# FFN gate and up, conv inputs, stick-breaking queries and keys and all gates with both activation parts as one 512-column operand

## The chip, the cores and the metric

The kernel runs on one core of one Trainium2 chip. The metric is device time in microseconds (us) of a launch; a profile is a separate, recorded execution. TensorE (PE) multiplies, with weight loads of its own (PEld); VectorE (DVE) and ScalarE (ACT) work element by element; GpSimd (POOL) does little here; SyncE (SP) and ScalarE issue the DMA transfers. Each engine takes its instructions in the order that was written into its stream when the program was built.

## What is computed

Two layers of an encoder on 256 rows of 1024 channels, all in float32. Each layer is an FFN, a mixer of three branches, and a second FFN, each followed by a residual and a layer norm:

```python
for l in range(2):
    x = layernorm(ALPHA * x + 0.5 * swiglu(x, ffn1_w_in[l], ffn1_w_out[l]))   # d_ff 2816
    x = layernorm(ALPHA * x + mixer(x, l))
    x = layernorm(ALPHA * x + 0.5 * swiglu(x, ffn2_w_in[l], ffn2_w_out[l]))

def swiglu(x, w_in, w_out):
    gate, up = split(x @ w_in)
    return (silu(gate) * up) @ w_out

def mixer(h):
    qa, ka, va, zb, xbc, dtb, qc, kc, vc, gpre = split(h @ w_in)
    o_a = diff_attention(qa, ka, va)              # two softmax maps a head
    o_b = mamba2(zb, silu(conv4(xbc)), dtb)       # state-space scan (SSD)
    o_c = stick_breaking(qc, kc, vc)
    return sum(sigmoid(gpre[r] + bias[r]) * (o[r] @ w_branch[r]) for r in 0, 1, 2) @ w_out
```

## The kernel before

Matrix products are made nearly in float32 from a faster format, float32r. A weight and an activation are each split into a high and a low part, and three products are added: high·high, high·low, low·high (`passes`). Weights come from DRAM 1 MB at a time (SP's queue, two `raw` buffers); ScalarE makes the high half (line 93), VectorE the low half (line 94), into six pairs of buffers `whi`, `wlo` (pool `wsp`). The transposed activations of a sub-layer lie in `xThi` and `xTlo`, 8 blocks k of 256 columns each.

`gemm_s` (line 131) makes a 128 x 256 piece of a transposed product: for each of 8 k, three matmuls of 256 columns with the weights as stationary operand. The FFN's `part_s` calls it for gate and up (4 FFNs x 10 blocks j x 2 x 2 halves f), `block_s` (line 372) for the six blocks of convolution inputs, for four blocks of queries and four of keys of the stick-breaking branch, and for 12 gate blocks a layer; `proj` calls it for the branch projections, with other activations. `block_a` (line 362) and `part_a` use xT the other way round, as the stationary operand, with 512 (line 368) or 256 (line 275) columns of weights moving. The FFN's output product (line 308) has `hhi`, `hlo` as stationary operand and 512 columns of weights moving.

Tiles are placed back to back in a partition. Those of weights, of `hhi` and `hlo` have sizes that are multiples of 64 floats, so they start on one grid of 256 bytes. `new_xT` takes a slice that begins `APART` = 48 floats into its tile, and the mixer's first small tile, `ss`, of 48 floats, shifts the mixer's tiles by as much.

PSUM has eight banks of 512 float32 columns: two in pool `gm`, four in `at`, two in `tp`. A bank is handed to the next user when the one before has read it. A `gemm_s` block takes one `gm` bank for both halves. The pool `at` holds the accumulators of the FFN's output and of the mixer's output, and in between the small products of the SSD stage (lines 452 to 521), the scores of stick-breaking (line 551) and of differential attention (line 629).

The order of instructions on each engine is set when the program is built, by a planner with costs of its own; it may move a block ahead of others if its buffers are free. In the SSD stage softplus gives `dt` and `dta` (lines 441 to 450); lines 454 to 457 make cumulated decays in an `at` bank; line 459 copies them, line 461 writes them to DRAM, line 464 reads them back to all partitions, one transfer of 1 MB for each half c of the rows; line 496 (16 times a half) and line 500 make decay factors, line 501 multiplies, and lines 507 and 512 are the matmuls.

## Time and profile before

| | |
|---|---|
| time, median of 3 runs | 1610.74 us (1610.71 to 1612.2) |
| profiled execution | 1617.37 us, span 1615.6 us, mean granted TensorE clock 0.994 |
| PE, PEld busy | 1591.5 us (99%), 1467.2 us (91%) |
| DVE, ACT busy | 984.7 us (61%), 848.4 us (53%) |
| matmuls, weight loads | 11282 each |

The span is the time from the first to the last instruction. A busy share says in how much of the span at least one instruction of the engine was running. The length of one matmul has its way through the array in it, so that matmuls that follow one another overlap, and what one costs is read from the distance of the starts. An arrow "<-" behind an idle time names what ended it.

### The profile page before, as it was taken

The page shows a single profiled execution, that of the slowest core. Times are in us where ns is not written, and L with a number is a line of the kernel's source. Part 1 is how long each engine was busy: PE and PEld are TensorE (multiplying, and loading weights), DVE is VectorE, ACT ScalarE, POOL GpSimd, SP SyncE. Part 2 cuts the span into 40 slices and gives each one's busy share as a digit, 9 for nine tenths or more (in the row PEclk, how much of TensorE's full clock was granted, in tenths as well). Part 3 has the DMA queues.
Part 4 walks back from the last instruction along what each step waited for, and adds up shares of the span by engine and source line. Part 5 has one row for each costly group of instructions (what it writes and reads, how often), then busy time and mean ns, then how long its engine had stood idle before and what let it go on. Part 6 is the DMA issues. An engine that isn't in the chain of part 4 may idle for free.

```text
span 1615.6 us, 26930 instructions
## 1 busy us (share of the span) xinstructions
PE 1591.5 (99%) x11282; PEld 1467.2 (91%) x11282; DVE 984.7 (61%) x1510; ACT 848.4 (53%) x1285; POOL 17.6 (1%) x28
## 2 busy tenths in 40 slices
PE   8999999999999999999999999999999999999998
PEld 8999899888799998999899998998788999999997
DVE  5555657767585556455655565777576855565454
ACT  5545356568675444444444453654676755444451
POOL 0000000000000000000000000000000000000000
PEclk9999999999999999999999999998999999999999
DMA  8665445543435674566445562663443356545651
GB/s 286 198 226 192 158 157 175 187 161 105 157 106 174 217 235 140 175 216 225 157 162 203 209 230 85 208 190 128 154 140 124 129 194 216 191 157 183 235 196 39
DMA packets 222117, 283.55 MB, mean 176 GB/s; under 512 B 8658, under 2 KB 185644, under 8 KB 221996
## 3 DMA queue, kind: packets, MB, share of 16 engines
q1 hardware_dynamic: 213676, 277.61, 51.0%
q10 hardware_dynamic: 8320, 4.23, 0.9%
q8 instruction: 88, 1.44, 0.4%
q14 instruction: 33, 0.27, 0.0%
HBM read 280.74 MB, written 1.08 MB: 174 GB/s over the span
## 4 chain that ended last, share of the span: by engine, by line
PE 95%; DVE 2%; DMA 2%; ACT 1%; issue 0%; POOL 0%; DVEq 0%; POOLq 0%; ACTq 0%
PE gm L135 52%; PE at L308 15%; PE gm L368 14%; PE gm L275 3%; PE at L730 2%; DMA t<-acd 2%; PE at L633 1%; PE at L507 1%; PE at L585 1%; PE at L577 1%; PE at L555 1%; PE tp L614 0%; DVE wlo L94 0%; DVE at L169 0%; DVE xt L160 0%; PE tp L145 0%
## 5 line engine op out<-in xcount | busy, mean ns | idle before, releaser
L94 DVE TENSOR_TENSOR wlo<-raw,whi 128x1024 fp32r<-128x1024 f32 x412 | 501.2, 1223 | 360.5 <-ACT whi L93 350.4
L93 ACT CAST whi<-raw 128x1024 fp32r<-128x1024 f32 x412 | 429.4, 1051 | 391.0 <-PE gm L135 229.4
L135 PE MATMUL gm<-xThi,whi 128*128 128x256 f32 x2112 | 595.1, 282 | 0.0
L135 PE MATMUL gm<-xTlo,whi 128*128 128x256 f32 x2112 | 594.8, 282 | 0.0
L135 PE MATMUL gm<-xThi,wlo 128*128 128x256 f32 x2112 | 594.2, 281 | 0.0
L135 PEld LDWEIGHTS gm<-xThi,wlo 128*128 128x128 f32 x2112 | 403.8, 191 | 1.8 <-issue 1.8
L135 PEld LDWEIGHTS gm<-xThi,whi 128*128 128x128 f32 x2112 | 398.4, 189 | 3.4 <-issue 1.8
L135 PEld LDWEIGHTS gm<-xTlo,whi 128*128 128x128 f32 x2112 | 397.9, 188 | 3.0 <-issue 1.6
L135 PE MATMUL gm<-t,whi 128*128 128x256 f32 x768 | 138.7, 282 | 0.0
L368 PE MATMUL gm<-whi,xThi 128*128 128x512 f32 x320 | 128.7, 402 | 1.2 <-ACT xThi L128 1.2
L94 DVE TENSOR_TENSOR wlo<-rawo,whi 128x1024 fp32r<-128x1024 f32 x68 | 83.1, 1225 | 72.8 <-ACT whi L93 69.7
L368 PE MATMUL gm<-whi,xTlo 128*128 128x512 f32 x320 | 126.9, 398 | 0.0
L368 PE MATMUL gm<-wlo,xThi 128*128 128x512 f32 x320 | 126.4, 395 | 0.0
L135 PEld LDWEIGHTS gm<-t,whi 128*128 128x128 f32 x768 | 117.2, 188 | 2.7 <-issue 2.7
L93 ACT CAST whi<-rawo 128x1024 fp32r<-128x1024 f32 x68 | 71.3, 1052 | 76.8 <-PE at L308 63.7
L135 PE MATMUL gm<-t,wlo 128*128 128x256 f32 x384 | 108.1, 281 | 0.0
L308 PE MATMUL at<-whi,hhi 128*128 128x512 f32 x256 | 78.9, 390 | 0.0
L308 PE MATMUL at<-wlo,hhi 128*128 128x512 f32 x256 | 78.9, 390 | 0.0
L308 PE MATMUL at<-whi,hlo 128*128 128x512 f32 x256 | 78.9, 390 | 0.0
L135 PEld LDWEIGHTS gm<-t,wlo 128*128 128x128 f32 x384 | 73.1, 190 | 0.0
L368 PEld LDWEIGHTS gm<-whi,xThi 128*128 128x128 f32 x320 | 60.3, 188 | 13.9 <-ACT xThi L128 2.1
L368 PEld LDWEIGHTS gm<-whi,xTlo 128*128 128x128 f32 x320 | 60.2, 188 | 13.5 <-DVE xTlo L129 0.9
(235 smaller groups left out, 1870.5 us busy)
## 6 DMA issues: line engine op xcount, KB each, us to landing
raw<-in_w_mix_in_dram SPq DMA_DIRECT2D x92, 1024.0 KB, 5.1
raw<-in_ffn_w_in_dram SPq DMA_DIRECT2D x85, 1024.0 KB, 4.9
rawo<-in_ffn_w_out_dram SPq DMA_DIRECT2D x44, 1024.0 KB, 7.2
raw<-in_w_branch_dram SPq DMA_DIRECT2D x24, 1024.0 KB, 5.5
raw<-in_w_mix_out_dram SPq DMA_DIRECT2D x8, 1024.0 KB, 6.2
t<-acd ACTq DMA_DIRECT2D x4, 1024.0 KB
rawo<-in_ffn_w_in_dram SPq DMA_DIRECT2D x2, 1024.0 KB
gb<-in_ln_g_dram SPq DMA_DIRECT2D x4, 512.0 KB
```

Source lines behind the costliest of these rows:

```text
L93: act.copy(out=hi, in_=src)
L94: dve.tensor_sub(out=lo, in0=src, in1=hi.bitcast(F32))
L135: pe.matmul(out=ps_out, lhsT=a[:, f:f + n], rhs=b[:, k, :], start=first, stop=(k == KT - 1 and i == 2))
L275: pe.matmul(out=ps[:, u * 256:(u + 1) * 256], lhsT=a[:, k, t * P:(t + 1) * P], rhs=c, start=first, stop=(k == KT - 1 and i == 2))
L308: pe.matmul(out=accs[t][h], lhsT=a[:, f, t * P:(t + 1) * P], rhs=c[:, h * 512:(h + 1) * 512], start=(j == 0 and f == 0 and i == 0), stop=( ...
L368: pe.matmul(out=ps, lhsT=a[:, k, t * P:(t + 1) * P], rhs=c, start=(k == 0 and i == 0), stop=(k == KT - 1 and i == 2))
L507: pe.matmul(out=py[:, 64 * h:64 * h + 64], lhsT=m[:, hh, :], rhs=xdt[:, c, 64 * hh:64 * hh + 64], start=True, stop=True)
L555: pe.matmul(out=pz[h][:, 0:S], lhsT=kcT[r, hp, 0:P], rhs=qcT[r, hp, :], start=True, stop=False, skip_group_check=True)
L577: pe.matmul(out=pz[h][:, 0:384], lhsT=trin, rhs=part[:, hs], start=False, stop=False, skip_group_check=True)
L585: pe.matmul(out=pz[c0][64 * h:64 * h + 64, 384:512], lhsT=vct[:, k, 64 * hh:64 * hh + 64], rhs=sp[:, 384 * h + c1:384 * h + c1 + P], start ...
L633: pe.matmul(out=pm[m][:, c:c + n], lhsT=qaT[r, h, t * P:(t + 1) * P], rhs=kaT[r, h, 0:n], start=True, stop=True, skip_group_check=True)
L730: pe.matmul(out=accs[t][h], lhsT=a[:, k, t * P:(t + 1) * P], rhs=c[:, h * 512:(h + 1) * 512], start=(k == 0 and i == 0), stop=(k == KT - 1 ...
```

## The change

`new_xT` makes one tile `xTj` in which, for each k, the 256 high columns and the 256 low columns stand side by side; it starts at offset `XPART` = 0, on the grid of the weights. A new `gemm_j` multiplies whi with all 512 columns at once, into a whole bank (left half high·high, right half high·low), and adds wlo times the 256 high columns to the left half. The two halves f of a block so take a bank each. ScalarE copies the right half out of PSUM (times a scale), VectorE adds the left half. The second bank comes from `tp` in the FFN's up and in the gates of branch 0, and from `at` in the convolution inputs, the queries, the keys and the other gates. What read PSUM directly (Silu, Tanh, the convolution's first tap, the product with up) reads the sum in SBUF. `block_a`, `part_a` and the dt product use the same tile as before, through its two views; `proj` still calls `gemm_s`.

```diff
@@ -31,6 +31,8 @@
 HOLD = 3
 
 APART = 48
+
+XPART = 0
 OFF_QA, OFF_KA, OFF_VA, OFF_ZB, OFF_XBC, OFF_DTB, OFF_QC, OFF_KC, OFF_VC, OFF_G = (
     0, 1024, 2048, 3072, 4096, 5632, 5648, 6672, 7696, 8720)
 NEG = -float(2 ** 100)
@@ -136,6 +138,14 @@
                           start=first, stop=(k == KT - 1 and i == 2))
                 first = False
 
+    def gemm_j(w, f, xT, ps):
+        for k in range(KT):
+            pe.matmul(out=ps, lhsT=w[k][0][:, f:f + P], rhs=xT[2][:, k, :], start=(k == 0), stop=(k == KT - 1),
+                      skip_group_check=True)
+            pe.matmul(out=ps[:, 0:S], lhsT=w[k][1][:, f:f + P], rhs=xT[0][:, k, :], start=False, stop=(k == KT - 1),
+                      skip_group_check=True)
+        return ps
+
 
     def transposed(t, xT):
         for q in range(2):
@@ -147,11 +157,9 @@
             split_act(xT[0][:, 4 * q:4 * q + 4, t * P:(t + 1) * P], xT[1][:, 4 * q:4 * q + 4, t * P:(t + 1) * P], pv)
 
     def new_xT():
-        def part(name):
-            whole = keep.tile([P, KT * S + 128], F32R, name=name)
-            return whole[:, APART:APART + KT * S].rearrange("p (k c) -> p k c", c=S)
-
-        return part("xThi"), part("xTlo")
+        whole = keep.tile([P, KT * 2 * S + 128], F32R, name="xTj")[:, XPART:XPART + KT * 2 * S]
+        both = whole.rearrange("p (k i c) -> p k i c", i=2, c=S)
+        return both[:, :, 0, :], both[:, :, 1, :], whole.rearrange("p (k c) -> p k c", c=2 * S)
 
     def layernorm(t, accs, coef, gb, sq):
         st = sm.tile([P, 5], F32, name="st")
@@ -289,15 +297,21 @@
                 spare = fresh and j == 1
                 wg = load_cols(w_in[l], j * 256, None, raws[0] if spare else None)
                 wu = load_cols(w_in[l], FF + j * 256, None, raws[1] if spare else None)
-                pg, pu = gm_tile(), gm_tile()
                 hT = new_h()
+                sg = fp.tile([P, 512], F32, name="h")
                 for f in range(2):
-                    gemm_s(pg[:, f * S:(f + 1) * S], wg, f * P, xT)
-                sg = fp.tile([P, 512], F32, name="h")
-                act.activation(out=sg, in_=pg, func=AF.Silu)
+                    ps = gemm_j(wg, f * P, xT, gm_tile())
+                    sf = sg[:, f * S:(f + 1) * S]
+                    act.copy(out=sf, in_=ps[:, S:2 * S])
+                    dve.tensor_add(out=sf, in0=sf, in1=ps[:, 0:S])
+                act.activation(out=sg, in_=sg, func=AF.Silu)
+                su = fp.tile([P, 512], F32, name="h")
                 for f in range(2):
-                    gemm_s(pu[:, f * S:(f + 1) * S], wu, f * P, xT)
-                dve.tensor_mul(out=sg, in0=sg, in1=pu)
+                    ps = gemm_j(wu, f * P, xT, tp_tile())
+                    sf = su[:, f * S:(f + 1) * S]
+                    act.copy(out=sf, in_=ps[:, S:2 * S])
+                    dve.tensor_add(out=sf, in0=sf, in1=ps[:, 0:S])
+                dve.tensor_mul(out=sg, in0=sg, in1=su)
                 split_act(hT[0], hT[1], sg.rearrange("p (f c) -> p f c", c=S))
                 return hT
 
@@ -369,12 +383,13 @@
                                       start=(k == 0 and i == 0), stop=(k == KT - 1 and i == 2))
                     evac(t, ps)
 
-            def block_s(c0, evac, w=wm):
-                ws = load_cols(w, c0)
-                ps = gm_tile()
+            def block_j(c0, dst, scale=1.0, second=at_tile):
+                ws = load_cols(wm, c0)
                 for f in range(2):
-                    gemm_s(ps[:, f * S:(f + 1) * S], ws, f * P, xT)
-                evac(ps.rearrange("p (f c) -> p f c", c=S))
+                    ps = gemm_j(ws, f * P, xT, second() if f else gm_tile())
+                    act.mul(out=dst[:, f, :], in_=ps[:, S:2 * S], mul=scale)
+                    dve.scalar_tensor_tensor(out=dst[:, f, :], in0=ps[:, 0:S], scalar=scale, in1=dst[:, f, :],
+                                             op0=ALU.mult, op1=ALU.add)
 
             ss = mp.tile([P, APART], F32, name="ss")[:, 0:2 * 8].rearrange("p (t h) -> p t h", h=8)
             zs = slot("t1", [P, NT, D])
@@ -406,14 +421,14 @@
             bcF = mp.tile([P, 4, S], F32, name="bcF")
             last_silu = [None]
             for cc in range(6):
-                def evac(ps, cc=cc):
+                def conv(cc=cc):
                     pad = mp.tile([P, 768], F32, name="w3", bufs=4)[:, 0:2 * 259].rearrange("p (f c) -> p f c", c=259)
                     ac = mp.tile([P, 768], F32, name="w3", bufs=4)[:, 0:512].rearrange("p (f c) -> p f c", c=S)
                     dve.memset(pad[:, :, 0:3], 0.0)
-                    act.copy(out=pad[:, :, 3:259], in_=ps)
+                    block_j(OFF_XBC + 256 * cc, pad[:, :, 3:259])
                     for f in range(2):
                         c = 2 * cc + f
-                        act.activation(out=ac[:, f, :], in_=ps[:, f, :], func=AF.Identity,
+                        act.activation(out=ac[:, f, :], in_=pad[:, f, 3:259], func=AF.Identity,
                                        scale=v[:, 36 + c:37 + c], bias=v[:, 48 + c:49 + c])
                         for i in range(3):
                             dve.scalar_tensor_tensor(out=ac[:, f, :], in0=pad[:, f, i:i + S],
@@ -429,7 +444,7 @@
                             pe.transpose(out=pt[:, t * S + f * P:t * S + (f + 1) * P],
                                          in_=ac[:, f, t * P:(t + 1) * P], identity=ident)
                     act.copy(out=xs[:, :, cc * 256:(cc + 1) * 256], in_=pt.rearrange("p (t c) -> p t c", c=256))
-                block_s(OFF_XBC + 256 * cc, evac)
+                conv()
 
 
             pt = tp_tile()
@@ -540,8 +555,8 @@
 
 
             for cc in range(4):
-                block_s(OFF_QC + 256 * cc, lambda ps: act.mul(out=qcT[:, 2 * cc:2 * cc + 2, :], in_=ps, mul=0.125))
-                block_s(OFF_KC + 256 * cc, lambda ps: act.copy(out=kcT[:, 2 * cc:2 * cc + 2, :], in_=ps))
+                block_j(OFF_QC + 256 * cc, qcT[:, 2 * cc:2 * cc + 2, :], 0.125)
+                block_j(OFF_KC + 256 * cc, kcT[:, 2 * cc:2 * cc + 2, :])
             for h in range(2):
                 block_a(OFF_VC + 512 * h, lambda t, ps: act.copy(out=vct[:, t, 512 * h:512 * h + 512], in_=ps))
 
@@ -691,12 +706,10 @@
 
             def gate(r, dp):
                 gt = slot(("bcF", "xde")[(r + dp) % 2 if r else dp % 2], [P, 2, S])
-
-                def evac(ps):
-                    for f in range(2):
-                        kk = 60 + 8 * r + 2 * dp + f
-                        act.activation(out=gt[:, f, :], in_=ps[:, f, :], func=AF.Tanh, scale=0.5, bias=v[:, kk:kk + 1])
-                block_s(OFF_G + 1024 * r + 256 * dp, evac)
+                block_j(OFF_G + 1024 * r + 256 * dp, gt, 1.0, at_tile if r else tp_tile)
+                for f in range(2):
+                    kk = 60 + 8 * r + 2 * dp + f
+                    act.activation(out=gt[:, f, :], in_=gt[:, f, :], func=AF.Tanh, scale=0.5, bias=v[:, kk:kk + 1])
                 return gt
 
             def proj(r, dp, o, gt, first, final=None):
```

The order of TensorE changes most behind layer 0's convolution inputs. Before, behind the SSD's decay products (lines 454 to 457, then 486 and 487), queries and keys follow (`gm_2969` and on):

```order
L457 MATMUL at_2657<-tri_sb_872,dta_2648 16x128 x2
L486 MATMUL at_2681<-bcF_2187 128x256
L487 MATMUL at_2681<-bcF_2187 128x128
L486 MATMUL at_2687<-bcF_2187 128x256
L487 MATMUL at_2687<-bcF_2187 128x128
L135 MATMUL gm_2969<-xThi_1945,wlo_2962 128x256
L135 MATMUL gm_2969<-xThi_1945,whi_2965 128x256
L135 MATMUL gm_2969<-xTlo_1946,whi_2965 128x256
```

180 rows of line 135 stand between that last line 487 and the first line 507. In the changed program (where lines 454, 457, 486, 487, 507 and 512 are now 469, 472, 501, 502, 522 and 527) the same place reads:

```order
L472 MATMUL at_2373<-tri_sb_787,dta_2364 16x128 x2
L501 MATMUL at_2397<-bcF_1975 128x256
L502 MATMUL at_2397<-bcF_1975 128x128
L501 MATMUL at_2403<-bcF_1975 128x256
L502 MATMUL at_2403<-bcF_1975 128x128
L522 MATMUL at_2428<-t3_1819,t4_1820 128x64 x8
L522 MATMUL at_2443<-t3_1819,t4_1820 128x64 x8
L522 MATMUL at_2474<-t3_1819,t5_1821 128x64 x8
L527 MATMUL at_2484<-xde_1823,cbm_2396 128x512
L522 MATMUL at_2494<-t3_1819,t5_1821 128x64 x8
L527 MATMUL at_2504<-xde_1823,cbm_2396 128x512
L143 MATMUL at_2584<-xTj_1734,whi_2557 128x512
```

Three first halves of queries and keys (`gm_2565`, `gm_2613`, `gm_2661`, 16 matmuls each) stand ahead of line 469, none between lines 502 and 522, and the second halves in `at` banks stand behind line 527; layer 1 has the same order.

On VectorE, the rows that lead up to the copy of the decays (line 459, now 474), before:

```order
L473 TENSOR_TENSOR t3_2031<-t2_2030,dt_2647 128x1024 x2
L94 TENSOR_TENSOR wlo_3082<-raw_3079,whi_3081 128x1024
L476 TENSOR_TENSOR t2_2030<-t2_2030,bvec0_894 128x1024
L94 TENSOR_TENSOR wlo_3086<-raw_3079,whi_3085 128x1024
L476 TENSOR_TENSOR t2_2030<-t2_2030,bvec0_894 128x1024
L459 COPY dtr_2663<-at_2657 16x256
```

and in the changed program, where line 391 adds a half-block's two parts:

```order
L464 SCALAR_TENSOR_TENSOR dt_2363<-dt_2363,dta_2364 128x32
L465 SCALAR_TENSOR_TENSOR dta_2364<-dt_2363,bvec0_809 128x32
L488 TENSOR_TENSOR t3_1819<-t2_1818,dt_2363 128x1024 x2
L391 SCALAR_TENSOR_TENSOR t6_1824<-gm_2661,t6_1824 128x256
L491 TENSOR_TENSOR t2_1818<-t2_1818,bvec0_809 128x1024
L474 COPY dtr_2379<-at_2373 16x256
```

Two splits of weights (line 94) are gone from there, and one add has come.

In the FFN the blocks of gate, up and output product follow one another as before, each half-block with 16 matmuls in place of 24.

## Rows read from the trace of the kernel before

**Rows 1.** The page, part 1: busy time of each engine, share of the span.

```profile
PE 1591.5 (99%) x11282; PEld 1467.2 (91%) x11282; DVE 984.7 (61%) x1510; ACT 848.4 (53%) x1285; POOL 17.6 (1%) x28
```

**Rows 2.** Groups by line and form: one pass of line 135, busy and mean ns.

```profile
L135 PE MATMUL gm<-xThi,whi 128*128 128x256 f32 x2112 | 595.1, 282 | 0.0
```

**Rows 3.** The timeline of PE in the first FFN: start, length, instruction.

```profile
29.55 0.28 PE L135 MATMUL gm<-xThi,whi 128*128 128x256 f32 x1
...
36.26 0.28 PE L135 MATMUL gm<-xThi,whi 128*128 128x256 f32 x1
```

**Rows 4.** The same in layer 0's convolution inputs.

```profile
243.42 0.28 PE L135 MATMUL gm<-xThi,whi 128*128 128x256 f32 x1
...
246.82 0.28 PE L135 MATMUL gm<-xThi,whi 128*128 128x256 f32 x1
```

**Rows 5.** The same in the FFN's output product.

```profile
188.56 0.39 PE L308 MATMUL at<-dhi,hhi 128*128 128x512 f32 x1
...
195.58 0.39 PE L308 MATMUL at<-dhi,hlo 128*128 128x512 f32 x1
```

**Rows 6.** The same in block_a, layer 0.

```profile
341.21 0.39 PE L368 MATMUL gm<-whi,xThi 128*128 128x512 f32 x1
...
348.08 0.39 PE L368 MATMUL gm<-whi,xThi 128*128 128x512 f32 x1
```

**Rows 7.** Busy us by stretch: PE, PEld, DVE, ACT, POOL; granted clock; DMA.

```profile
20.00:180.00 160.00, 160.00 (x1181) 152.24 (x1181) 90.34 (x99) 80.69 (x93) 0.00 (x0) 1.00 0.63 218
221.00:257.00 36.00, 36.00 (x319) 35.91 (x318) 26.70 (x48) 25.07 (x39) 0.00 (x0) 1.00 0.62 191
1093.90:1104.00 10.10, 10.10 (x50) 10.10 (x49) 10.10 (x15) 3.08 (x5) 0.00 (x0) 0.50 0.32 105
```

**Rows 8.** Groups by line: PSUM read of 256 columns by ACT, by DVE.

```profile
L538 DVE SCALAR_TENSOR_TENSOR t<-tp,pvec,t 128x256 fp32r<-128x256 f32 x16 | 7.0, 477 | 11.4 <-ACT t L537 11.4
...
L537 ACT ACTIVATE t<-tp,pvec 128x256 fp32r<-128x256 f32 x16 | 6.7, 473 | 6.6 <-PE tp L534 6.6
```

**Rows 9.** Timeline of PE around the state-space stage, layer 0.

```profile
270.30 0.52 PE L454 MATMUL at<-dta,tri_sb 128*128 128x16 f32 x4
...
272.70 0.39 PE L487 MATMUL at<-bcF 128*128 128x128 f32 x2
...
294.98 3.79 PE L507 MATMUL at<-t,t 128*128 128x64 f32 x32 [1.48 <-DVE t L501]
```

**Rows 10.** Timeline of DVE there.

```profile
267.47 0.19 DVE L450 SCALAR_TENSOR_TENSOR dta<-dt,bvec 128x32 f32<-128x32 f32 x1
267.58 2.35 DVE L473 TENSOR_TENSOR t<-t,dt 128x1024 f32<-128x1024 f32 x2
...
274.39 0.41 DVE L459 COPY dtr<-at 16x256 f32<-16x256 f32 x1
...
285.08 3.23 DVE L496 TENSOR_SCALAR t<-t,ac 128x128 f32<-128x128 f32 x16 [1.47 <-DMA t<-acd]
...
291.94 1.85 DVE L496 TENSOR_SCALAR t<-t,ac 128x128 f32<-128x128 f32 x9 [2.50 <-DMA t<-acd]
293.71 1.22 DVE L501 TENSOR_TENSOR t<-t,cbm 128x1024 f32<-128x1024 f32 x1
```

**Rows 11.** Timeline of ACT and its DMA queue there.

```profile
275.86 1.05 ACT L93 CAST whi<-raw 128x1024 fp32r<-128x1024 f32 x1 [5.24 <-PE gm L135]
275.87 0.35 ACTq L461 DMA_DIRECT2D acd<-dtr  x1
...
278.53 2.13 ACTq L464 DMA_DIRECT2D t<-acd  x2
```

**Rows 12.** Timeline of PE in the state-space stage, layer 1.

```profile
1092.83 6.17 PE L507 MATMUL at<-t,t 128*128 128x64 f32 x32 [1.59 <-DVE t L501]
...
1099.12 0.41 PE L135 MATMUL gm<-xThi,whi 128*128 128x256 f32 x1
...
1103.38 0.41 PE L135 MATMUL gm<-xThi,wlo 128*128 128x256 f32 x1
```

## The prediction

> **What bounds the kernel now.** I read the page first. TensorE is busy in 99% of the span [rows 1], its 11.3 thousand matmuls in one unbroken line: a microsecond that it works less, or stands still more, is a microsecond of the time, wherever it is. VectorE and ScalarE, at 61% and 53% [rows 1], have room, so I price their work only where TensorE waits for it.
>
> Since busy times of pipelined matmuls overlap, the cost of one is not its mean of 282 ns [rows 2] but the distance between starts, read off the timeline. The three-pass product (whi·hi, whi·lo, wlo·hi for each k, line 135) has two paces. In the FFN 57 matmuls start in 6.71 us, one every 117.7 ns [rows 3]; in the convolution inputs 30 start in 3.40 us, one every 113.3 ns [rows 4]. Of 512-column matmuls, 31 steps of the FFN's output product take 7.02 us, 226.5 ns each, twice 113.3 [rows 5]; 30 steps of the mixer's block_a take 6.87 us, 229.0 ns each [rows 6]. So 0.443 ns a column is the floor seen here, and something adds 4.4 ns in the FFN's three-pass product and 2.5 ns in block_a. What differs between these is placement: hhi, hlo and the output weights lie on one 256-byte grid, while xThi and xTlo lie 48 floats off the grid of the weights. The convolution inputs are off it too and run at the floor [rows 4], so the grid is one way to it, not the only one.
>
> **Gains.** The change makes of each k two matmuls in place of three: 512 columns, then 256. The columns stay the same, 768; a weights load and a start go. With xTj on the grid I take 226.5 for the 512 [rows 5] and 113.3 for the 256 [rows 4]: 226.5 + 113.3 = 339.8 ns, against 3 x 117.7 = 353.1, that is 13.3 ns for a triple. Of the 2112 triples [rows 2] 1280 are in the FFNs (4 x 10 j, gate and up, 2 f, 8 k): 17.0 us. Of the mixers' 832 the 448 of convolution, queries and keys are at 3 x 113.3 = 339.9 already and gain nothing; the 384 of the gates I read at the FFN's pace, 5.1 us. block_a now has its stationary operand on the grid: 960 x 2.5 ns = 2.4 us; line 275, read at 117.7 against 113.3 ns [rows 3, 4], 384 x 4.4 ns = 1.7 us. Together 26.2 us. No row shows a 256-column matmul on the grid with a full weights load beside it. If each load goes on costing 4.4 ns, a pair is 348.6 ns and the gain 4.5 ns x 1280 = 5.8 us. The bounds are 5.8 and 26.2; I take the upper one, since the 512-column rows on the grid show no excess at all.
>
> The Trainium skill (TensorE: Matmul & The Clock Gate, Back-to-back issue gap) gives a warm matmul N/2.4 + 2.5 ns, a fixed cost per instruction. By it a triple would be 327.6 ns, a pair 325.0, and the gain an estimated 2.5 ns x 2112 = 5.3 us. The trace differs: over N/2.4 512 columns lie 13.2 ns [rows 5] and 256 lie 6.6 ns [rows 4], an excess that grows with the columns. The sum goes by the rows.
>
> **Evacuations.** Each half-block now adds a ScalarE copy of 256 columns from PSUM and a VectorE add; the nearest rows are 473 and 477 ns [rows 8]. An FFN step j (96 matmuls of 117.7 ns and 24 of 226.5, 16.7 us [rows 3, 5]) gets four of each, 1.9 us on either engine; over 160 us of FFN VectorE is busy 90.3 and ScalarE 80.7 [rows 7], so they rise from 56% and 50% to some 68% and 62%, under TensorE, and the four banks of gate and up are wanted again only a step later. In the convolution stage VectorE has 26.7 of 36 us [rows 7] and gets 12 x 0.48 = 5.7 more, 32.4 of about 35: still covered, but barely. I cost these at nothing; with the cover gone it is 2 to 3 us a layer.
>
> **The wait that is added.** The second half of a queries or keys block now takes its PSUM bank from the pool `at`, which the state-space (SSD) stage uses ahead of it, so the block can't be finished before that stage. The rows of the order show it: before, 180 matmuls of line 135 stand between line 487 and the first line 507, which is 20.4 us at 113.3 ns, the stretch 273.1 to 293.5 in the trace [rows 9], and TensorE waits 1.48 us. In the changed program nothing stands there: line 502 is followed by line 522, which waits for decays that come over DRAM. How long, from rows:
>
> From the end of line 450 (267.66) VectorE does line 473 twice (2.35 us), one new add (0.48), line 476 (1.18) and the copy 459 (0.41) [rows 10]: 4.4 us. Before, two splits stood in between. The write to DRAM then goes at once; before, it stood behind a cast that waited 5.24 us for TensorE, and went 1.07 us after the copy [rows 11]. From its issue to the first line 496 is 275.87 to 285.08, 9.2 us [rows 10, 11]. Sixteen of line 496 take 3.23 us and line 501 takes 1.22. Sum 18.1 us, in which TensorE has lines 454 to 487, 270.30 to 273.09 [rows 9], 2.8 us. **It idles 15.3 us.** The second chunk's decays are there 6.86 us after the first's [rows 10]; its 13 + 1 operations put the second group of matmuls 10.7 us after that first landing, while the first group ends 6.4 after it: 4.3 us more idle, or 1.0 if the broadcast, without weight loads beside it, lands 3.3 us sooner; I take 3. Ahead of line 469 the filler (three half-blocks of 2.7 us) about covers the softplus chain; I take 0.5. That is 18.8 us a layer against 1.48 now: 17.3 more, 34.6 for both. All queued behind the waiting line 522 on TensorE, the half-blocks, the rest of queries and keys, then block_a, comes that much later, and nothing later has slack to give it back [rows 1]. Bounds: 13 to 22 us a layer.
>
> **The clock.** In layer 1 the granted clock was 0.50, the 1.2 GHz level, for 10.1 us from 1093.9 [rows 7], after a wait of 1.59 us: 32 records of line 507 took 6.17 us against 3.79 in layer 0, and 20 matmuls of line 135 took 4.26 us (213 ns each) against 2.27 [rows 9, 12]. That costs some 4.6 us now, in one layer of two. After 15 us of idle I expect it in both, through the SSD's 9.7 us of small matmuls (part of it inside the waits above) and the first dense work behind: 6 us a layer, 12 - 4.6 = 7.4 us more. Bounds: -4.6 (no drop at all) and 15.
>
> **Sum**, against the profiled execution: 1617.4 - 26.2 + 34.6 + 7.4 = 1633.2 us, 15.8 more. The median of the runs is 1610.7, 6.6 under the profiled one; I carry the difference over: **1626.5 us**.
>
> **Rivals.** *The pace doesn't follow the grid*: every load keeps its 4.4 ns, the gain is 5.8 us, and the time 1610.7 + 42.0 - 5.8 = 1646.9. For it: the FFN and the convolution inputs have the same placement and yet differ [rows 3, 4], so placement alone doesn't set the pace. Against it: on the grid the pace is twice the floor to 0.1 ns [rows 5]. The fixed cost that the Trainium skill gives (TensorE: Matmul & The Clock Gate, Back-to-back issue gap) would by an estimate end at about the same place. *The wait is short*: the broadcasts, alone on the DMA engines, land 3.3 us sooner, the second gap closes to nothing and the clock holds: idle 18.8 - 3.3 - 3 = 12.5 a layer, 11 more than now, and no drop in either layer: 22 - 4.6 - 26.2 = -8.8, 1601.9. It decides below 13.1 us of added wait and clock a layer. Against it: the chain of lines 459, 461, 464, 496, 501 is serial, and 15 us of idle hardly leave the clock alone. *The gates starve the differential attention too*: their second halves also take `at` banks, which the scores of the heads hold; TensorE is filled there with gates and projections now. If eight half-blocks (21.8 us a layer) come too late for half of their gaps, it adds 10 us a layer: 1646.5. Against it: first halves and projections stay early in the order.
>
> **How the numbers follow.** The forecast gets 0.62, pace 0.14, short wait 0.12, gates 0.10, others 0.02. The forecast's own range is 1614 to 1640 (gain 15 to 26, wait 15 to 20 a layer). To leave out no more than 2 in 10 it goes to 1606 and 1646. A difference of 0.2% (3.2 us) is about what a measurement of this kernel can tell from none. Faster: most of the short wait, 0.11. Within: 0.08, where its parts mix with the forecast. Slower: 0.81.
>
> **What would show it.** FFN starts 340 ns apart per pair (348 by the pace rival); block_a at 226.5; TensorE idle of 15 us before the first line 522 and 1 to 4 before the second, in both layers, put down to VectorE or the DMA; clock 0.50 there in both layers; no TensorE waits over 1 us in the FFNs. The prediction is wrong if the order's gap is filled by a chain under 12 us, or if the pair runs under 330 ns.

## The result, and the profile after

The changed kernel takes 1664.6 us (median of 4 runs, 1663.7 to 1667.8) against 1611.5 us of the kernel before on the same chip: ratio 1.033, 95% interval 1.031 to 1.035. It is slower, as forecast, but by 53 us where 15.8 were forecast, and outside the range. The profiled execution took 1664.81 us, with a span of 1662.7. Part 1 of its page, to be laid beside [rows 1]:

```profile
PE 1610.6 (97%) x9170; PEld 1382.5 (83%) x9170; DVE 1093.7 (66%) x1774; ACT 930.6 (56%) x1523; POOL 17.5 (1%) x28
```

2112 matmuls are gone, yet the busy time of TensorE has risen by 19 us, and its idle share of the span from 1% to 3%. Stage by stage (each from its first transpose of the residual stream to that of the next stage, us):

| stage | before | after |
|---|---|---|
| FFN 1, 2, 3, 4 | 191.2, 191.0, 188.6, 198.9 | 191.4, 192.7, 189.1, 199.3 |
| mixer, layer 0 and 1 | 418.2, 423.1 | 441.8, 444.3 |

The four FFNs, which were to give 17 us, give nothing (2.8 us longer). The mixers lose 44.8 us.

**The pace.** Timeline of PE in the changed kernel: first a stretch of the first FFN, 30 pairs from the first row to the second, then one of layer 0's convolution inputs, 9 pairs. They answer to [rows 3, 4]:

```profile
117.78 0.40 PE L143 MATMUL gm<-xTj,whi 128*128 128x512 f32 x1
...
128.38 0.40 PE L143 MATMUL tp<-xTj,whi 128*128 128x512 f32 x1
...
235.50 0.40 PE L143 MATMUL gm<-xTj,whi 128*128 128x512 f32 x1
...
238.63 0.39 PE L143 MATMUL at<-xTj,whi 128*128 128x512 f32 x1
```

10.60 us over 30 are 353.3 ns a pair in the FFN, to the nanosecond what three products of 117.7 took [rows 3]. In the convolution inputs 3.13 us over 9 are 347.8 ns, where three products took 3 x 113.3 = 339.9 [rows 4]. The pair at 339.8 ns, on which 22 of the 26.2 us of gain were built, is nowhere in this trace. In the pairs of the FFN the next start comes some 236 ns behind the 512-column product and 117 behind the 256-column one, in the convolution inputs 230 to 232 and 115 to 117: both are over the 226.5 and 113.3 of my sum. The two smaller gains part ways, in the next rows: block_a, whose stationary operand is now on the grid, makes 75 steps in 17.00 us, 226.7 ns against the 229.0 of [rows 6] (in the mean of all its steps 227.9 against 229.4); line 283 (line 275 before), also there, makes 18 in 2.16 us, 120.0 ns, slower than the 117.7 at which I had it.

```profile
339.37 0.39 PE L382 MATMUL gm<-wlo,xTj 128*128 128x512 f32 x1
...
356.37 0.39 PE L382 MATMUL gm<-wlo,xTj 128*128 128x512 f32 x1
```

```profile
17.68 0.28 PE L283 MATMUL gm<-wlo,xTj 128*128 128x256 f32 x1
...
19.84 0.28 PE L283 MATMUL gm<-wlo,xTj 128*128 128x256 f32 x1
```

**The wait.** Timelines of PE, of VectorE and of ScalarE's DMA queue around the state-space (SSD) stage of layer 0, answering to [rows 9 to 11] (the last column is the idle time before, and what ended it):

```profile
269.53 0.38 PE L502 MATMUL at<-bcF 128*128 128x128 f32 x2
283.36 10.84 PE L522 MATMUL at<-t,t 128*128 128x64 f32 x48 [13.45 <-DVE t L516]
...
298.47 0.80 PE L143 MATMUL at<-xTj,whi 128*128 128x512 f32 x1
```

```profile
270.62 0.41 DVE L474 COPY dtr<-at 16x256 f32<-16x256 f32 x1
...
278.95 3.22 DVE L511 TENSOR_SCALAR t<-t,ac 128x128 f32<-128x128 f32 x16 [2.70 <-DMA t<-acd]
282.09 1.22 DVE L516 TENSOR_TENSOR t<-t,cbm 128x1024 f32<-128x1024 f32 x1
```

```profile
271.06 0.35 ACTq L476 DMA_DIRECT2D acd<-dtr  x1
```

The chain is the one foretold: copy, write to DRAM, decays back (278.95 - 271.06 = 7.9 us, 9.2 were taken from before), sixteen subtractions, the mask, and only then TensorE. The idle is 13.45 us, not 15.3. Behind it TensorE has 68 small products in four groups, for 15.1 us. Until the clock rises they start 213 ns apart, against 110 to 112 at the full clock, with one pause of 0.3 us where I had put a second gap of 3. The list of waits of the whole execution has both layers in its first row, and nothing new behind it that is longer than 2.4 us in all:

```profile
PE at L522 <- DVE t L516: 26.8, 2, 13.5
...
PE tp L673 <- ACT cbm L672: 2.4, 2, 1.2
```

The same stage by windows, columns as in [rows 7], answering to its last row. First the idle, then the groups of SSD products:

```profile
266.97:283.37 16.40, 2.90 (x19) 2.34 (x19) 11.91 (x32) 2.76 (x5) 0.00 (x0) 0.68 0.47 129
283.37:297.80 14.43, 14.33 (x65) 13.14 (x66) 11.35 (x27) 3.56 (x6) 0.00 (x0) 0.54 0.01 2
```

The granted clock is at 0.50, the lower level of 1.2 GHz, from 272.8 to 296.7 in layer 0 and for 27.3 us from 1098.8 in layer 1.

**What a layer lost.** The queries and keys products that TensorE ran inside the SSD stage, by the windows of their line, before (columns: length, PE, PEld, clock, DMA, GB/s) and after:

```profile
270.30:306.60 36.30, 25.21 (x213) 24.29 (x211) 1.00 0.61 192
```

```profile
266.97:298.47 31.50, 0.00 (x1) 0.03 (x1) 0.62 0.25 68
```

Before, the stage took 36.3 us of which TensorE spent 25.2 on 213 products of queries and keys. Now it takes 31.5 us without one of them, and the 25.2 us are to be done behind it: 25.2 - (36.3 - 31.5) = 20.4 us. From the layer's start to the start of stick-breaking the two timelines differ by just that (-3.0 us up to the cumulative sums, +23.4 from there); the differential attention and the gates add 3.2, together the 23.6 us of layer 0.

### The profile page after: what moved, and what is told of

Read it like the earlier page. It is cut to its first block, busy times and chain, and to the rows that moved or that the text cites. A ratio compares the mean times of both kernels' runs of the same rounds, so it can differ in the third digit from the quotient of the medians.

```text
span 1662.7 us, 23327 instructions
## 1 busy us (share of the span) xinstructions
PE 1610.6 (97%) x9170; PEld 1382.5 (83%) x9170; DVE 1093.7 (66%) x1774; ACT 930.6 (56%) x1523; POOL 17.5 (1%) x28
## 4 chain that ended last, share of the span: by engine, by line
PE 94%; DVE 3%; DMA 1%; ACT 1%; issue 0%; POOL 0%; SPq 0%; DVEq 0%; POOLq 0%; ACTq 0%
PE gm L143 15%; PE at L322 14%; PE gm L382 14%; PE tp L143 10%; PE gm L137 8%; PE gm L145 7%; PE tp L145 5%; PE at L143 5%; PE gm L283 3%; PE at L145 3%; PE at L743 2%; PE at L522 2%; PE at L648 1%; PE at L600 1%; PE at L592 1%; DMA t<-acd 1%
## 5 line engine op out<-in xcount | busy, mean ns | idle before, releaser
L143 PE MATMUL gm<-xTj,whi 128*128 128x512 f32 x1056 | 376.9, 397 | 0.0
L145 PE MATMUL gm<-xTj,wlo 128*128 128x256 f32 x1056 | 297.4, 282 | 0.0
L143 PE MATMUL tp<-xTj,whi 128*128 128x512 f32 x704 | 250.2, 397 | 0.0
L143 PEld LDWEIGHTS gm<-xTj,whi 128*128 128x128 f32 x1056 | 198.3, 188 | 45.5 <-issue 0.7
L382 PE MATMUL gm<-whi,xTj 128*128 128x512 f32 x640 | 204.1, 396 | 0.7 <-ACT xTj L130 0.7
L145 PEld LDWEIGHTS gm<-xTj,wlo 128*128 128x128 f32 x1056 | 199.4, 189 | 1.9 <-issue 0.3
L145 PE MATMUL tp<-xTj,wlo 128*128 128x256 f32 x704 | 197.6, 281 | 0.0
L143 PEld LDWEIGHTS tp<-xTj,whi 128*128 128x128 f32 x704 | 132.2, 188 | 32.4
L145 PEld LDWEIGHTS tp<-xTj,wlo 128*128 128x128 f32 x704 | 133.0, 189 | 0.0
L143 PE MATMUL at<-xTj,whi 128*128 128x512 f32 x352 | 127.0, 400 | 0.8 <-ACT w L658 0.8
L95 ACT CAST whi<-rawo 128x1024 fp32r<-128x1024 f32 x68 | 71.3, 1051 | 19.2 <-PE at L322 15.1
```

The source lines that it names most:

```text
L95: act.copy(out=hi, in_=src)
L143: pe.matmul(out=ps, lhsT=w[k][0][:, f:f + P], rhs=xT[2][:, k, :], start=(k == 0), stop=(k == KT - 1), skip_group_check=True)
L145: pe.matmul(out=ps[:, 0:S], lhsT=w[k][1][:, f:f + P], rhs=xT[0][:, k, :], start=False, stop=(k == KT - 1), skip_group_check=True)
L382: pe.matmul(out=ps, lhsT=a[:, k, t * P:(t + 1) * P], rhs=c, start=(k == 0 and i == 0), stop=(k == KT - 1 and i == 2))
```

## The experiments

Times are medians, and each ratio is against the kernel before, run beside the kernel named.

### The wait: banks, order, engines, clock

**Only the banks undone, and only the banks done.** First the edit in the changed kernel (the keys likewise), then that in the kernel before, in block_s, whose bank is then at_tile for queries and keys and gm_tile else:

```diff
-                block_j(OFF_QC + 256 * cc, qcT[:, 2 * cc:2 * cc + 2, :], 0.125)
+                block_j(OFF_QC + 256 * cc, qcT[:, 2 * cc:2 * cc + 2, :], 0.125, gm_tile)
```

```diff
-                ps = gm_tile()
+                ps = bank()
```

> The changed kernel, only the second PSUM tile of the stick-breaking queries and keys blocks comes from the same pool as their first (gm) and no longer from the pool that the SSD tiles use, so that these blocks can stand in the program between the cumulative sums and the SSD products again. Theory 1 (the wait at the SSD and the half-rate clock behind it made the loss): the idle of 13.4 us ahead of the scores in each layer shrinks to at most 3 us, the granted clock stays at 1.00 there in layer 0, the stretch from the cumulative sums to stick-breaking falls from 92.0 us by 20 to 24 us in each layer, and the time is 1618 to 1626 us, still above the kernel before because the pairs' pace is unchanged at 352 ns. Theory 2 (the two-engine evacuations and the pace made the loss, the wait only uncovered slack): the idle shrinks but the time stays above 1645 us.

> The kernel before, only the PSUM tile of the stick-breaking queries and keys blocks comes from the pool of the SSD tiles (at). No operand, pace or evacuation changes. Theory 1 (bank choice alone makes the wait and the slow clock): idle of 13 to 14 us ahead of the scores in both layers, a half-rate stretch of some 24 us behind it, 20 to 24 us a layer, time 1651 to 1660 us. Theory 2 (the wait is short without the other parts of the change): under 1625 us.

The kernel before with nothing but its queries and keys on the other pool takes 1668.6 us, ratio 1.032 (1.029 to 1.036): the bank alone makes a loss as large as that of the whole change. (It moves more than the change did: there only the second half of each block takes an `at` bank, here the whole block.) Its list of waits in layer 0's stage:

```profile
PE at L507 <- DVE t L501: 11.8, 1, 11.8
PE at L454 <- DVE dta L450: 7.6, 1, 7.6
```

The changed kernel with these banks put back takes 1645.9 us, 1.019 (1.016 to 1.022): by the ratios some 23 us better, not 40. By its number that is the second theory's side, by 1 us; by its reason it is neither, since a wait is left, in the right place:

```profile
PE at L522 <- DVE t L516: 8.0, 1, 8.0
PE gm L143 <- DVE t L391: 1.1, 1, 1.1
```

The idle is down from 13.45 to 8.0 us and not to 3. In the order of that program 67 matmuls of the pairs stand between line 502 and the first SSD product, some 11.8 us at 176 ns, where before there were 180 of 113.3 ns, 20.4 us. A half-block of pairs fills a bank by itself, so that two banks of gm hold half as much of this work ahead; that is my reading of the order. The clock is at 0.50 there as well, for 13.7 us in layer 0 and 20.5 in layer 1.

**Queries and keys as before, the rest changed** (the keys likewise; block_s and its gm tile are those of the kernel before).

```diff
-                block_j(OFF_QC + 256 * cc, qcT[:, 2 * cc:2 * cc + 2, :], 0.125)
+                block_s(OFF_QC + 256 * cc, lambda ps: act.mul(out=qcT[:, 2 * cc:2 * cc + 2, :], in_=ps, mul=0.125))
```

> The changed kernel, but the stick-breaking queries and keys keep three products of 256 columns, one PSUM tile of gm and one evacuation on ScalarE, as before the change; conv inputs, gates and FFN keep the joint operand. Theory 1 (the whole loss hangs on the queries and keys: their banks, and the second evacuation on VectorE that queues behind the SSD's work): no idle over 2 us ahead of the scores, granted clock 1.00 there in layer 0, mixer stretches of 418 to 425 us as before, time 1612 to 1622 us. Theory 2 (conv inputs and gates cost the mixer as well): mixer stretches of 428 us or more, time above 1630 us.

1616.5 us, ratio 1.0040 (1.0025 to 1.0054), mixers 420.0 and 420.3 us, and no idle in the stage: the row of its window there has TensorE busy for all of 52 us at clock 1.00.

```profile
258.00:310.00 52.00, 52.00 (x425) 50.55 (x424) 43.59 (x86) 27.78 (x42) 0.00 (x0) 1.00 0.57 185
```

So some 47 of the 53 us (1.033 down to 1.004) hang on the queries and keys. And the rest of the change, conv inputs, gates and all FFNs on pairs, gives no gain: it stands 7 us behind. In this kernel the three products of queries and keys read the operand on the grid, 6 triples between these rows, 2.16 us or 120.0 ns a product:

```profile
268.74 0.40 PE L137 MATMUL gm<-xTj,whi 128*128 128x256 f32 x2
...
270.90 0.40 PE L137 MATMUL gm<-xTj,whi 128*128 128x256 f32 x2
```

Before the change these 768 took 114.7 ns in the mean (stretches of 113.4 and of 117.8), so they make 4 of the 7 us.

**Is it the evacuation on VectorE?** In the kernel before, half of each queries or keys block is evacuated by VectorE:

```diff
+            def two(dst, cc, ps, scale):
+                act.mul(out=dst[:, 2 * cc, :], in_=ps[:, 0, :], mul=scale)
+                dve.tensor_scalar(out=dst[:, 2 * cc + 1, :], in0=ps[:, 1, :], scalar1=scale, scalar2=None, op0=ALU.mult)
```

> The kernel before, but the evacuation of the stick-breaking queries and keys is shared: ScalarE takes the first 256 columns of a block, VectorE the other 256; banks, operands and products as before. Theory 1 (what is left of the loss when the banks are undone, some 12 us a layer, comes from an evacuation on VectorE that queues behind the SSD's work): idle of some microseconds ahead of the first SSD product or inside the queries and keys, and 8 us or more a layer, time 1625 to 1640 us. Theory 2 (the pairs' shorter cover and their place in the order make it): within 4 us of the kernel before.

1616.9 us, 1.0013 (0.9996 to 1.0030): no loss to be seen, so that an evacuation on VectorE doesn't by itself make what is left. The pairs' evacuation in two steps, ScalarE and then VectorE, was not tried alone; TensorE's waits for it with the banks put back are 2.4 us in all. The shorter cover remains, read from the order and not tested by itself.

**Is the slow clock a loss?** Extra products, their result unused, keep TensorE at work in the wait (first kernel, below, with FILL 12). The second kernel has three more ahead of each later group of SSD products; the order puts 15 into the wait and three each ahead of the second and the fourth group:

```diff
                     py = at_tile()
+                    if c == 0 and g == 0:
+                        idle = tp_tile()
+                        for i in range(FILL):
+                            pe.matmul(out=idle, lhsT=cbm[:, 0, 0, :], rhs=zs[:, 0, 0:512], start=True, stop=True)
```

> The changed kernel with 12 extra products (fp32, 512 columns, about 0.9 us each, their result unused) between the scores and the first SSD product of each layer, in the middle of the 13.4 us in which TensorE idles. Nothing that the kernel computes is changed. Theory 1 (the idle lets the clock fall to half, and the half-rate stretch of 24 to 27 us is a loss of its own): the clock stays at 1.00 there, and the time falls by 8 to 20 us, to 1645 to 1657 us, although TensorE does more work. Theory 2 (the half-rate stretch lies beside VectorE's work and costs nothing): within 3 us of 1664.6. If the added products outlast the wait, up to 3 us a layer slower.

> The changed kernel with extra products (fp32, 512 columns, unused result) both in the wait ahead of the first SSD product (15) and between the SSD's groups of products (3 ahead of the second and of the fourth), since with the wait alone filled the granted clock still fell to half during the groups. Nothing that the kernel computes is changed. If the half-rate stretch is a loss of its own, the clock stays at 1.00 through the groups and the time falls by 6 us or more below 1663. If the SSD's end is set by VectorE and the clock lies beside it, the time stays within 3 us of the changed kernel (or rises by what the added products outlast the waits, up to 4 us a layer) while the half-rate stretch goes.

The first takes 1663.3 us, 1.0337 (1.0321 to 1.0352), the second 1662.1, 1.0318 (1.0294 to 1.0341), against the change's own 1.033. In the first the clock still fell, to 0.50 for 17.1 us from the SSD products on, in each layer. Windows and the end of the stage in the second:

```profile
270.00:285.00 15.00, 13.51 (x34) 6.18 (x33) 10.51 (x35) 2.77 (x5) 0.00 (x0) 1.00 0.51 141
285.00:299.00 14.00, 14.00 (x82) 10.19 (x80) 11.43 (x23) 4.28 (x8) 0.00 (x0) 1.00 0.01 1
```

```profile
298.67 0.79 PE L144 MATMUL at<-xTj,whi 128*128 128x512 f32 x1
```

The idle is filled, the clock stays at 1.00 throughout, and the next dense product starts at 298.67 against 298.47. That doesn't show the slow clock to be free, because the added products stand in TensorE's order ahead of the SSD's own. First the last products of the stage in this kernel, then the last in the changed kernel, on TensorE and on VectorE:

```profile
293.85 2.74 PE L523 MATMUL tp<-t,cbm 128*128 128x512 f32 x6
296.43 1.89 PE L526 MATMUL at<-t,t 128*128 128x64 f32 x16
```

```profile
293.99 2.02 PE L527 MATMUL at<-xde,cbm 128*128 128x512 f32 x2
295.80 2.31 PE L522 MATMUL at<-t,t 128*128 128x64 f32 x16
```

```profile
289.24 1.21 DVE L516 TENSOR_TENSOR t<-t,cbm 128x1024 f32<-128x1024 f32 x1
...
294.24 0.69 DVE L524 TENSOR_TENSOR t<-at,t 128x512 f32<-128x512 f32 x1 [1.86 <-PE at L522]
```

In the changed kernel VectorE has the last group's operand ready at 290.45 (289.24 + 1.21), TensorE comes to it at 295.80, and VectorE waits for TensorE. So TensorE at the lower clock sets the end of the stage. By an estimate from the times at which VectorE has the four groups ready (283.3, 287.0, 288.7, 290.45) and from the full pace of 110 ns a product, the next dense product would start some 4.5 us earlier in layer 0. Layer 1 takes 2.5 us longer than layer 0 up to the stick-breaking, its first pairs at the lower clock included, which makes 7 there: 11 to 12 us in both layers, where the kernel before had 4.9 in one. With the fill VectorE has the last operand ready at 291.12, and TensorE is held until 296.4, at the end by three added products. The fill took back most of what the clock gave. No run shows the clock's price by itself. The Trainium skill (TensorE: Matmul & The Clock Gate, HAM oscillation — how this bites in real kernels) warns that idling drops the clock and that the work behind pays. The trace agrees: 48 SSD products take 10.84 us behind the idle, where 32 took 3.79 before [rows 9].

### The pace: grid, interruptions, program

**The grid taken from the pairs, and given to the three products.** The changed kernel's operand off the grid, and the kernel before with its parts on it (in a third kernel 128 bytes off, from 32 in place of 0):

```diff
-XPART = 0
+XPART = 48
```

```diff
-            return whole[:, APART:APART + KT * S].rearrange("p (k c) -> p k c", c=S)
+            return whole[:, 0:KT * S].rearrange("p (k c) -> p k c", c=S)
```

> The changed kernel with the joint operand moved by 192 bytes, off the grid of the weights; nothing else. If the grid sets the pace of a pair (my prediction's reason), the 512-column product slows from its mean of 235 ns by 4 ns or more, a pair from 352 to 357 ns or more, and the time rises by 8 us or more (some 2100 pairs). If the grid does not set it, the pair stays at 350 to 354 ns and the time within 3 us of 1664.6.

> The kernel before, only its two activation parts are moved by 192 bytes onto the grid of the weights; still three products of 256 columns. If the grid sets the pace, the product falls from 117.7 to about 113.3 ns in the FFN (the stretch of an FFN falls by some 4 us each, 17 us in all) and the time is about 1590 us. If it does not, the FFN products stay at 117.7 ns and the time within 3 us of 1611.5.

> The kernel before, its two activation parts placed 128 bytes off the grid of the weights in place of 192. At 192 bytes the FFN products took 117.7 ns, on the grid 120.0. If the distance from the grid sets the pace, the product stands between or below these throughout; if only being on the grid or off it counts, 117.7 ns in the FFN again and 1609 to 1616 us.

Off the grid the changed kernel takes 1673.1 us, 1.0351 (1.0308 to 1.0394), which doesn't stand clear of the change's own 1.033. Its pairs in the FFN stand at 352.5 ns (4 pairs in the first two rows below), as on the grid. In the convolution inputs they stand at 353.3 (9 pairs in the next two rows), where the pairs on the grid took 347.8; no stretch off the grid is under 351. So the grid gives a pair some 6 ns in much of the mixers and nothing in most of the FFN. The kernel before on the grid is slower, 1629.1 us, 1.0085 (1.0051 to 1.0118). Its FFN products make 33 steps between the last two rows, 3.95 us, 119.7 ns, not 113.3, and its convolution inputs stand at 120.0 too:

```profile
127.74 0.40 PE L143 MATMUL tp<-xTj,whi 128*128 128x512 f32 x1
...
129.15 0.40 PE L143 MATMUL tp<-xTj,whi 128*128 128x512 f32 x1
...
234.82 0.40 PE L143 MATMUL gm<-xTj,whi 128*128 128x512 f32 x1
...
238.00 0.40 PE L143 MATMUL at<-xTj,whi 128*128 128x512 f32 x1
```

```profile
102.81 0.28 PE L135 MATMUL gm<-xThi,whi 128*128 128x256 f32 x1
...
106.76 0.28 PE L135 MATMUL gm<-xThi,whi 128*128 128x256 f32 x1
```

128 bytes off the grid it is no better (1628.1 us, 1.0114, and 118.6 to 120 ns). For a moving operand of 256 columns the grid was the wrong place.

Compared at the same place, the pair does save something: on the grid three products take 360 ns and a pair 347 to 353; 192 bytes off it three take 340 to 353 and a pair 353. The change paid with the one for the other, since it moved the operand onto the grid as well. The Trainium skill (TensorE: Matmul & The Clock Gate, Step-by-step: what each phase is for) gives TensorE two read ports, so that loading the next weights takes nothing from the running matmul. Here the same loads and matmuls run at paces from 113.3 to 120 ns, by where the operands lie and by what went before, and that account has no place for this; which part of the path they share no run shows.

**A state that an interruption sets.** In the kernel before the two paces change only where something else was put between: after the two transposes of line 437, for instance, and back after the cumulative sums, in both layers at nearly the same places. The probe puts transposes of the identity ahead of the FFN's parts (first FFN: one ahead of each; second: two; third: one ahead of parts 2 and 5; fourth: one of 32 columns; an excerpt):

```diff
+                n = PROBE[call[0]]
+                for _ in range(n[1] if n[0] == "all" or j in n[0] else 0):
+                    if n[2] == P:
+                        pe.transpose(out=pg[:, 0:P], in_=ident, identity=ident)
+                    else:
+                        pe.transpose(out=pg[:, 0:32], in_=ident[0:32, :], identity=ident[0:32, 0:32])
```

> The kernel before with extra small transposes of the identity ahead of the gate product of the FFN parts: in the first FFN one of 128 columns in each part, in the second two, in the third one in the second and the fifth part only, in the fourth one of 32 columns in each part. They write PSUM that the product overwrites; nothing that is computed changes. Theory 1 (the pace of the 256-column products is a state that such an interruption sets and that holds until the next): products stand at either 113.3 or 117.8 ns from one interruption to the next, and at least one of the four FFNs shows parts at 113.3 ns where the kernel before shows 117.8 in all. Theory 2 (pace follows from operands' addresses alone): 117.8 ns in all four FFNs as before, whatever is put between. The transposes themselves cost about 0.2 us each, some 32 of them, 7 us.

Timeline of PE in two neighbouring parts of its first FFN, the same kind of products 16 us apart, 33 steps in each pair of rows:

```profile
102.75 0.28 PE L138 MATMUL gm<-xThi,whi 128*128 128x256 f32 x1
...
106.49 0.28 PE L138 MATMUL gm<-xThi,whi 128*128 128x256 f32 x1
...
118.80 0.28 PE L138 MATMUL gm<-xThi,wlo 128*128 128x256 f32 x1
...
122.69 0.28 PE L138 MATMUL gm<-xThi,wlo 128*128 128x256 f32 x1
```

3.74 us is 113.3 ns a step, 3.89 us is 117.9, with the 24 products of the FFN's output (line 308, now 318) and one transpose between. Within a row of products that nothing interrupts, up to 178 of them, the pace never changed. Behind transposes it came out either way. Output products are an interruption too, and behind them alone it always came out slow: in the eight traces with three products and the operand 192 bytes off, 198 times of 198, six of them after a stretch at the better pace. So the FFNs of the kernel before, with output products ahead of nearly every part, show 117.8 ns. The fourth FFN here stood at 117.8 in all its parts.

**Can it be steered?** Transposes only where the probe had switched to the better pace, without (first diff) and with four more in each mixer's branch products (second, in proj); and the probe's idea on the pairs of the kernel with three-product queries and keys:

```diff
-PROBE = (("all", 1, P), ("all", 2, P), ((2, 5), 1, P), ("all", 1, 32))
+PROBE = (((1, 2, 3), 1, P), ((1, 2), 2, P), ((), 0, P), ((1, 2), 2, P))
```

```diff
+                if r == 1:
+                    pe.transpose(out=ps[:, 0:P], in_=ident, identity=ident)
```

> The kernel before with extra transposes of the identity only where the probe's trace showed the products of the FFN drop to 113.3 ns and stay there: one each ahead of the parts 1, 2 and 3 of the first FFN, two each ahead of the parts 1 and 2 of the second and the fourth, none in the third. Theory 1 (a state that an interruption sets, that the same instruction sequence sets again, and that holds until the next interruption): first and second FFN run at 113.3 ns from their third or second part to the end, 3 to 4 us shorter each than 191; the third at 113.3 ns if its state comes from the sequence ahead of it; time 1599 to 1608 us, 0.2 to 0.8 per cent faster than the kernel before. Theory 2 (the state falls by chance in each execution): the FFNs show either state without relation to the probe's, time within 4 us of the kernel before.

> As the kernel with extra transposes in the FFN, and one more ahead of each branch product of the second branch in the mixer (four in a layer), where the kernel before ran at 117.8 ns to the mixer's end. Theory 1: the state after each of them is one of the two and holds, and some of the 90 us to the mixer's end run at 113.3 ns, 1 to 3 us less in a layer; the time is between 1595 and 1608 us. Theory 2 (chance): no relation, time within 4 us of the kernel before.

> The kernel with the joint operand in FFN, conv inputs and gates and three products in the stick-breaking queries and keys, with one extra transpose of the identity ahead of each gate product of the FFN. Theory 1 (a pair on the grid has its own two states, 230 + 117 and 236 + 117.7 ns, and no state reaches the floor of the three products): the pair stands at 347 or 354 ns after each interruption and never under 345 ns. Theory 2 (the pair's floor of 340 ns is there, only not visited): some parts stand at 338 to 342 ns.

The steered kernels take 1613.6 and 1614.5 us, 1.0003 (0.9987 to 1.0019) and 1.0008 (0.9989 to 1.0027): nothing won. In the first FFN of the first of them the part behind the third transpose ran at the better pace (33 steps in 3.74 us, first two rows) and the next part, with only output products ahead of it, at the slow one (41 steps in 4.83 us, 117.8 ns), as did nearly all the rest. I had read the probe as if the pace would hold from part to part, but there each part had a transpose of its own.

```profile
52.08 0.28 PE L138 MATMUL gm<-xThi,wlo 128*128 128x256 f32 x1
...
55.82 0.28 PE L138 MATMUL gm<-xThi,wlo 128*128 128x256 f32 x1
...
66.83 0.28 PE L138 MATMUL gm<-xThi,whi 128*128 128x256 f32 x1
...
71.66 0.28 PE L138 MATMUL gm<-xThi,wlo 128*128 128x256 f32 x1
```

The pairs on the grid show states of their own: behind most transposes of the first, second and fourth FFN they stand at some 347 ns (the rows below: 11 pairs in 3.81 us, 346.4 ns), in the third at 353, and nowhere lower. Behind output products alone, in the changed kernel, they stand at 353.

```profile
152.74 0.39 PE L143 MATMUL gm<-xTj,whi 128*128 128x512 f32 x1
...
156.55 0.39 PE L143 MATMUL gm<-xTj,whi 128*128 128x512 f32 x1
```

**The same two programs profiled again.**

> The kernel before, unchanged, profiled once more. If the pace of the FFN products is set by the program (instructions, addresses), every stretch stands at the same of the two paces as in its first profile: 117.8 ns in all four FFNs. If it falls by the moment at which an interruption comes, some stretches stand at the other pace.

> The kernel with extra transposes in the FFN, unchanged, profiled once more. Set by the program: the parts of the first FFN stand again at 117.8, 117.8, 113.3, 113.3, 113.3, 113.3, 117.8, 113.3, 117.8, 113.3 ns in this order. Set by the moment: another order.

The kernel before shows 117.8 ns in the four FFNs again and 113.3 in the convolution inputs; of its long stretches one, the last of queries and keys in layer 0, changed. In the probe's first FFN the parts 2 to 6 show the same pace again, the first and the last four each the other one; in its second FFN they repeat. So the program mostly settles the state, the moment sometimes; what picks it behind a transpose is open. In its second profile the kernel before has no half-rate stretch in layer 1 and a second mixer of 418.3 us, against 423.1 in the profile that I had read.

## Why the prediction was wrong

- **What bounds it**: right. TensorE is at 97%, and what it stands still more has come through to the end.
- **The gain, 26.2 us: the step that failed.** I took 226.5 + 113.3 ns for a pair from [rows 4, 5] and gave the grid the credit. On the grid the pair takes 347 to 353 ns (230 to 236 and 115 to 117), against 340 to 353 of the three products where they lay before, so that nothing is left of the gain. The rows were true and badly joined: 113.3 was one of two states of a 256-column product 192 bytes off the grid, where the FFN's output products set the other; on the grid it takes 120.0, and 226.5 belongs to the output product. Even the lower bound of 5.8 us was too good: the kernel without the queries and keys stands 7 us behind, 4 of them their 120 ns, about nothing for the pairs. Two readings were off as well: queries and keys stood at 114.7 ns in the mean, not at 113.3, and the gates at 116.1, not at 117.7. Of the terms only block_a's came near its price (2.3 ns a product in the rows, 1.5 in the mean, 2.5 forecast). The rival that the pace doesn't follow the grid, at 0.14, came nearest, though its 1646.9 is 18 us short and the pairs of the mixers do follow the grid. Its own warning, that FFN and convolution inputs lie alike and run differently, was the sign to follow.
- **The wait, 17.3 us a layer, and the clock, 7.4 us**: right in place and chain, and near in sum: 42.0 for both layers against 38.3 (20.4 in layer 0, 17.9 in layer 1, up to the stick-breaking). In its parts: in layer 0 the idle grew by 12 us, 5 under the 17.3, and the other 8.4 are SSD groups that TensorE works off at the lower clock, and between which it formerly had queries and keys. The clock fell in both layers as foretold; by the estimate above it cost 11 to 12 us where 12 were foretold, but they are inside the 38.3 and no run shows them alone. That leaves some 4 us a layer that I had not priced and that made up for the idle taken too long: so far the sum agrees by luck. What was to be priced is the work that loses its cover, less what the stage gets shorter.
- **Evacuations at nothing**: right where it was tried. The list of waits of the whole execution has none of TensorE on them in the FFNs, and the shared evacuation of queries and keys made no difference.
- **Gates that starve the differential attention**: 10 us a layer feared, 3.2 measured there, not separated further.
- **From profile to median, -6.6 us**: wrong. That execution's excess was mainly its one half-rate stretch (423.1 us for the second mixer, 418.3 in the kernel's second profile), and the changed kernel's profiled time is its median. Without it the same sum gives 1633.

With what was measured put in, 1617.4 + 38.3 + 2.8 in the FFNs + 6.5 behind the start of stick-breaking in the two layers = 1665.0, against a profiled 1664.8.

None of the kernels tried beats the kernel before.

## What to carry to other kernels

Ask of a moved PSUM tile what work its bank let run early: the loss is the cover that ends, some 20 us a layer here, for a change of one pool's name. A pace read in one stage is not the property of the one feature that you see there: if two stages with that feature run differently, look for what else differs before you build a gain on it, or try the feature alone. Whether a fallen clock costs is read from what waits for what behind the idle, not from a busy share; and a filler that holds the clock up must not stand ahead of the work that the clock is held up for.

## What I had not expected of the hardware

- Products of 256 fp32r columns with a weights load each, their moving operand 192 bytes off the weights' grid, have two steady paces, 113.3 and 117.8 ns. The pace changes only where another instruction stands between, and behind 24 products of 512 columns it was 117.8 each time; those stay at 226.5.
- The activations' place against the weights matters and not in the sense of alignment: 192 bytes off the weights' grid 113.3 or 117.8 ns, 128 off 118.6 to 120, on it 120, for the same three products.
- A pair of 512 and 256 columns on the grid has two paces too, 347 and 353 ns; 192 bytes off the grid it showed 353 alone.
- After 13 us of idle the SSD's small products started 213 ns apart, not 110, and with that TensorE, not VectorE, set the end of their stage.
